# A hybrid attention and state-space trunk step: scaled scores with their extreme in one VectorE pass, and rectified squares of three places on ScalarE

## The chip, the cores and the metric

The kernel runs on one core of a Trainium2 chip. The time is what the device takes for one execution, in microseconds (us), from the first to the last instruction and what lies around them. TensorE (PE) multiplies matrices into PSUM, VectorE (DVE) and ScalarE (ACT) read and write PSUM and SBUF, GpSimd (POOL) works in SBUF, and SyncE (SP) issues most transfers.

## The reference, cut to what matters

One layer of a hybrid encoder: 1024 prompt frames and 64 frames of a running stream, 1,088 columns together, width 1024. Everything is float32; matmuls run on a high part and a low remainder of each operand, three products for one.

```
xn = rmsnorm(x); c_q, c_kv, k_pe, u = split(xn @ w_in)
attention (8 heads, block-causal): s = q k^T * scale; p = softmax(s); out = p v
state space over u: complex diagonal scan, GELU, sigmoid gate
h = x + concat(rmsnorm(attn), rmsnorm(ssm)) @ w_out
h = h + square(relu(rmsnorm(h) @ w_up)) @ w_down       # 1024 -> 4096 -> 1024
y = rmsnorm(h)
```

## The kernel before, in words

The work goes through stages: input projection and state space (to about 330 us), attention of the prompt (334 to 500 us), the gate and the output projection, the norm before the MLP, the up projection (to about 1000 us), the down projection and the final norm.

**Attention.** The loop at line 1299 goes over 64 items (h, i): 8 heads, 8 blocks of 128 queries, in the order `ORD`. Block i sees W = 128 (i + 1) keys, so W is 128 to 1024. `scores(h, i)` (line 1169) makes the scores in a PSUM tile `S` of two banks, of which the pool has two (tag `a`). VectorE then takes the row's maximum over W columns (line 1187) and multiplies that one column by `qsn`, the negative scale of the row (line 1188); the result `nm` is the bias of ScalarE's exponential (line 1190), which reads `S` with the row's scale `qsc`, writes the tile `P` and sums the row. When ScalarE has read `S`, the tile is free for the scores after next. Three items later `back` transposes `P` on TensorE; ScalarE copies the high part out of PSUM (line 1200) and VectorE takes the remainder (`PTl`, line 1201 by the helper at line 51); `values` multiplies with v.

**The up projection** is done by a scheme of seven products instead of eight (`SEQ = "XYXYXZX"`), which add up in three PSUM tiles X, Y and Z. The 4096 rows are cut into 16 sets. `up_evac` (line 1759) empties a tile after each of the seven steps: steps 0 to 2 are copies by ScalarE; steps 3 to 5 add the tile to what was copied (line 1765, VectorE) and then rectify and square it in SBUF (`relu2`, line 1752); step 6 rectifies from PSUM on ScalarE (line 1769), and then line 1773 on VectorE reads the tile in PSUM once more for the square. With `on_act` the squares are two ScalarE instructions (lines 1754 and 1755, and 1771), without it one VectorE instruction, `stt` (line 333). Before the change `on_act` is true for set 2 alone.

The columns come in two chunks of 544. Sets 0 and 1 do their first chunk early (`up_first`) and their second in `up_pair`, ahead of set 9 (`MID`); these tiles are `Xp`, `Yp`, `Zp` and their evacuations have 272 columns. `up_set` does every other set with 544 columns at a time. After a set `up_sums` (line 1775) makes four sums on VectorE and stores seven blocks to HBM on SyncE's queue. That queue, in order, also has the loads of the weights (`wr`, line 1579) and the loads of the stored blocks for the down projection (`rr`, line 1800). The weights go from `wr` through sums (`ws`, VectorE, lines 1604 to 1610) to a high part (ScalarE, line 1618) and a remainder (`wl`, GpSimd, line 51).

**What sets the order.** Parts inside `manual_schedule` (the gate, the start of the MLP up to set 2, the end) keep the order in which they are written. Everything else, attention and sets 3 to 15 among it, is ordered for each engine by a planner when the program is built, from its own estimate of what each instruction takes. Each engine then works through its list in order.

Of the kernel before, what the change touches and what calls it, by code (L numbers as in the profile page):

```python
# [13 lines left out]
AF = mybir.ActivationFunctionType  # L14
ALU = mybir.AluOpType
# [14 lines left out]
def tile_hybrid_step(ctx: ExitStack, tc: tile.TileContext, I: dict, O: dict):  # L30
    nc = tc.nc
    act, dve, pool, pe = nc.scalar, nc.vector, nc.gpsimd, nc.tensor
# [6 lines left out]
    def pg(shape, name, dt=F32):  # L39
        return pages.tile(shape, dt, tag="pg", name=name)  # L40
# [3 lines left out]
    def psb(name):  # L44
        return ps1.tile([128, 512], F32, tag="b", name=name)

    def psa(name):
        return ps1.tile([128, 2, 512], F32, tag="a", name=name, bufs=2)
# [18 lines left out]
    rs = const.tile([128, 9, 8], F32, name="rs")  # L67
    negm = const.tile([128, 9, 8], F32, name="negm")
    qsc = const.tile([128, 9], F32, name="qsc")
    qsn = const.tile([128, 9], F32, name="qsn")  # L70
# [261 lines left out]
    def stt(out, a, s, b, o1, o2):  # L332
        dve.scalar_tensor_tensor(out, a, s, b, op0=o1, op1=o2)  # L333
# [388 lines left out]
    for mt in range(6):  # L722
# [17 lines left out]
        if mt == 4:  # L740
            rt = pg([128, 2, NT], "rot")
# [187 lines left out]
    def head_rows(h):  # L929

        if h % 2 == 0:
            return slice(0, 64), 64, slice(0, 96)
        return slice(64, 128), 32, slice(0, 128)
# [9 lines left out]
    NMP = 0; STP = 1; VHP = 2  # L943
# [16 lines left out]
    for j in range(2):  # L960
        for b in range(2):
            rn, c = slice(64 * b, 64 * b + 64), slice(64 * b, 64 * b + 64)
# [72 lines left out]
    heads, h, wait, v_done = [], 0, 0, False  # L1035
# [59 lines left out]
    for i in range(4):  # L1095
        ps = psb(f"pvc{i}")
        c = slice(128 * i, 128 * i + 128)
# [43 lines left out]
    def p2(shape, dt, name, tag, bufs):  # L1141

        if tag in early:
            return early.pop(tag)
        return ph2.tile(shape, dt, name=name, tag=tag, bufs=bufs)
# [23 lines left out]
    def scores(h, i):  # L1169
        _, _, rk = head_rows(h)  # L1170
        b = h % 2
        W = 128 * (i + 1)
        S = psb(f"S{h}_{i}")[:, None, :] if i in SB else psa(f"S{h}_{i}")
        q = slice(128 * i, 128 * i + 128)
        for bank in range((W + 511) // 512):
            c0 = 512 * bank
            n = min(512, W - c0)
            o = S[:, bank, :n]
            last = c0 + n == W
            pe.matmul(o, lhsT=qT_h[b][rk, q], rhs=kT_h[rk, b, c0:c0 + n], start=True, stop=False)  # L1180
            pe.matmul(o, lhsT=qT_h[b][rk, q], rhs=kT_l[rk, b, c0:c0 + n], start=False, stop=False)
            pe.matmul(o, lhsT=qT_l[b][rk, q], rhs=kT_h[rk, b, c0:c0 + n], start=False, stop=not last)
            if last:
                pe.matmul(S[:, bank, n - 128:n], lhsT=mrow[:, 0:128], rhs=mrow[:, 128:256], start=False, stop=True)
        Sf = S.rearrange("p a c -> p (a c)")[:, 0:W]
        nm = negm[:, i, h:h + 1]
        dve.tensor_reduce(nm, Sf, axis=mybir.AxisListType.X, op=ALU.max)
        (pool if NMP and i < NMP else dve).tensor_scalar(nm, nm, qsn[:, i:i + 1], None, op0=ALU.mult)
        Pt = p2([128, NP], F32, f"P{h}_{i}", "P", 3)
        return Pt, lambda: act.activation(Pt[:, 0:W], Sf, AF.Exp, bias=nm, scale=qsc[:, i:i + 1], accum_out=rs[:, i, h:h + 1])  # L1190

    def transposes(h, i, Pt, PTh, PTl):
        c = slice(128 * (i % 2), 128 * (i % 2) + 128)
# [90 lines left out]
    def flush():  # L1284
        for g in list(later):
            try:
                next(g)
            except StopIteration:
                later.remove(g)
        while ready:  # L1290
            h, i = ready.pop(0)
            if i % 2 == 1:
                values(h, i // 2, *PTs.pop((h, i // 2)), vhs[h])
            if h % 2 == 1 and i == ORD[7]:
                later.append(norm_pair(h // 2))
# [3 lines left out]
    for n, (h, i) in enumerate(items):  # L1299
# [12 lines left out]
        Pt, ex = scores(h, i)  # L1312
# [18 lines left out]
    def rq(shape, name, dt=F32):  # L1331
        return ph3.tile(shape, dt, name=name, tag="rq", bufs=6)
# [103 lines left out]
    NH, NC = NT // 2, NT // 4  # L1436
# [36 lines left out]
    def pump(n=1):  # L1473
        for _ in range(n):
            for g in list(live):
                try:
                    next(g)
                except StopIteration:
                    live.remove(g)
# [87 lines left out]
    MID = 9  # L1567
# [61 lines left out]
    def w_next():  # L1629
        ahead.extend([x for x in [next(wst, None)] if x is not None])  # L1630

    def w_take():
        w = ahead.pop(0)
        w_next()
        return w
# [11 lines left out]
    def step():  # L1647

        todo = later[:]
        later.clear()  # L1650
        for z in todo:
            z()
        pump()
# [92 lines left out]
    def up_product(w, o, i, c, first):  # L1746
        for kt in range(4):
            l = [w[:, x, 128 * kt:128 * kt + 128] for x in range(2)]
            r = [Hop[c][i][:, x, kt] for x in range(2)]
            three(o, l, r, first and kt == 0, kt == 3)  # L1750

    def relu2(z, on_act):
        if on_act:
            act.activation(z, z, AF.Relu)
            act.activation(z, z, AF.Square)
        else:
            stt(z, z, 0.0, z, ALU.max, ALU.mult)

    def up_evac(i, o, z, on_act=False):

        if i in (0, 1, 2):
            act.copy(z(*((0, 0), (1, 1), (1, 0))[i]), o)
        elif i in (3, 4, 5):
            z = z(*((1, 0), (1, 1), (0, 0))[i - 3])
            dve.tensor_tensor(z, o, z, op=ALU.add)  # L1765
            relu2(z, on_act)
        else:
            z = z(0, 1)
            act.activation(z, o, AF.Relu)
            if on_act:  # L1770
                act.activation(z, z, AF.Square)
            else:
                stt(z, o, 0.0, z, ALU.max, ALU.mult)

    def up_sums(b, parts):

        g, k = b // 2, b % 2
        rc, re = rq([128, 2, NH], f"rc{b}"), rq([128, 2, NH], f"re{b}")
        out = rd[g][k]
        for cs, (b11, b21, b12, b22) in parts:  # L1780
            c_, e_ = rc[:, :, cs], re[:, :, cs]
            dve.tensor_tensor(c_[:, 0], b12, b11, op=ALU.subtract)
            dve.tensor_tensor(c_[:, 1], b22, c_[:, 0], op=ALU.subtract)
            dve.tensor_tensor(e_[:, 0], b22, b12, op=ALU.subtract)
            dve.tensor_tensor(e_[:, 1], b21, c_[:, 1], op=ALU.subtract)
            for n, z in ((0, b11), (5, b21), (3, b22)):
                nc.sync.dma_start(out[:, n, cs], z)
            yield
        nc.sync.dma_start(out[:, 1:3], rc)
        nc.sync.dma_start(out[:, 4:7:2], re)  # L1790
# [55 lines left out]
    def up_pair():  # L1846

        rt = [rq([128, 2, 2, NC], f"rb{s_}") for s_ in range(2)]
        made = {}
        for i, x in enumerate(SEQ):  # L1850
            first = x not in made
            if first:
                made[x] = psa(f"{x}p1")
            for s_ in range(2):
                up_product(w_take(), made[x][:, s_, :NC], i, 1, first)
            for s_ in range(2):
                up_evac(i, made[x][:, s_, :NC], lambda k, q: rt[s_][:, k, q])
            pump()
        return rt

    def up_set(b, held=False):
        rt = [rq([128, 2, NH], f"r{x}{b}") for x in "ab"]
        made = {}
        for i, x in enumerate(SEQ):
            w = ahead.pop(0) if held else w_take()
            first = x not in made
            if first:
                made[x] = psa(f"{x}{b}")
            for c in range(2):
                up_product(w, made[x][:, c, :NC], i, c, first)  # L1870
                if held:
                    flush()
                    if c == 0:
                        w_next()
                    step()
            late.append(lambda i=i, x=x: up_evac(i, made[x][:, :, :NC], lambda k, q: rt[k][:, q].rearrange(
                "p (c n) -> p c n", c=2), held))
            if not held:
                flush()
                pump()  # L1880
            if b == 15 and i:
                next(tst)
        flush()
        for _ in up_sums(b, [(slice(0, NH), [t[:, q] for t in rt for q in range(2)])]):
            pass
# [22 lines left out]
    for b in range(3, MID):  # L1908
        up_set(b)
    rt = up_pair()  # L1910
    live.append(pair_sums())
    for b in range(MID, 16):
        up_set(b)
# [30 lines left out]
    for g in range(8):  # L1944
        for jp in range(2):
            if g == 7 and jp == 1:
                break
            made = {}
# [24 lines left out]
    made = [{}, {}]  # L1973
# [319 lines left out]
```

## Time and profile before

| | |
|---|---|
| median of three runs | 1365.03 us (1363.34 to 1367.58) |
| the profiled execution | 1365.45 us, span 1363.3 us |
| mean granted TensorE clock | 0.982 |
| PE busy | 1300.7 us, 95% |
| DVE busy | 1008.7 us, 74% |
| ACT busy | 668.9 us, 49% |
| POOL busy | 641.2 us, 47% |
| moved by DMA | 151.38 MB, mean 111 GB/s |

Busy times are those of one profiled execution; PE's matmuls are pipelined, and the ends that its rows show are modelled. A bracket behind a row of the timeline is how long the engine was idle just before it and what released it.

### The profile page before, as it was taken

Reading aid. Unit: us, or ns where it says so; the run is one execution under the profiler, and the core shown is the slowest. Engines: PE = TensorE matmul, PEld = TensorE weight load, DVE = VectorE, ACT = ScalarE, POOL = GpSimd, SP = SyncE. Lnnn points to the kernel's source line nnn. Section 1 sums busy time; section 2 is a strip of 40 time slices with the busy share of each in tenths; the row PEclk is TensorE's granted clock in tenths of the full one; section 3 lists DMA queues with packets and bytes.
Section 4 is the critical chain, followed back from the end, with each engine's and each line's share of the span. In section 5 each row is a group of like instructions: output and inputs, shape, how many; then the busy total and the mean of one; then the engine's idle time right before and its main releaser. Section 6 shows DMA issues by size and latency. Waiting matters only on the chain.

```text
span 1363.3 us, 24889 instructions
## 1 busy us (share of the span) xinstructions
PE 1300.7 (95%) x9576; PEld 1261.3 (93%) x9576; DVE 1008.7 (74%) x1653; ACT 668.9 (49%) x1333; POOL 641.2 (47%) x626
## 2 busy tenths in 40 slices
PE   6999999989999899999899999899989999999996
PEld 6999998978888789999899999899989999999996
DVE  7679779867788765639965667657587878888756
ACT  6576667756788765214542324232355433343333
POOL 3647556341545516200554546445445446453554
PEclk9999999999999899999999999999999999999998
DMA  6111111210244315124234424443577445664103
GB/s 223 65 41 42 34 30 32 90 49 8 40 86 79 70 65 161 32 96 134 83 115 152 177 97 156 174 169 122 209 252 227 126 154 167 183 180 127 63 1 132
DMA packets 81286, 151.38 MB, mean 111 GB/s; under 512 B 10128, under 2 KB 28816, under 8 KB 81168
## 3 DMA queue, kind: packets, MB, share of 16 engines
q1 hardware_dynamic: 76464, 144.78, 33.5%
q10 hardware_dynamic: 4704, 5.01, 1.1%
q8 instruction: 76, 1.25, 0.4%
q14 instruction: 42, 0.34, 0.1%
HBM read 98.66 MB, written 41.40 MB: 103 GB/s over the span
## 4 chain that ended last, share of the span: by engine, by line
PE 46%; DVE 7%; DMA 4%; POOL 3%; issue 2%; ACT 1%; SPq 0%; DVEq 0%; POOLq 0%; ACTq 0%
PE X L1742 4%; PE X L1744 4%; PE X L1743 4%; PE dX L1742 3%; PE dX L1743 3%; PE dX L1744 3%; PE pw L1494 2%; PE pw L1496 2%; PE pw L1495 2%; POOL wl L51 2%; PE Y L1743 2%; PE Y L1742 2%; PE Y L1744 2%; DMA wr<-in_w_dn_dram 2%; PE dY L1742 2%
## 5 line engine op out<-in xcount | busy, mean ns | idle before, releaser
L51 POOL TENSOR_TENSOR wl<-wr,wl 128x512 fp32r<-128x512 f32 x127 | 196.7, 1557 | 157.3 <-ACT wl L1618 95.3
L51 POOL TENSOR_TENSOR wl<-ws,wl 128x512 fp32r<-128x512 f32 x95 | 146.8, 1546 | 235.6 <-ACT wl L1618 231.2
L1618 ACT CAST wl<-ws 128x512 fp32r<-128x512 f32 x96 | 59.6, 622 | 196.4 <-DVE ws L1606 98.2
L1742 PE MATMUL dX<-to,wl 128*128 128x272 f32 x512 | 149.0, 291 | 3.2 <-DVE q L1939 2.4
L1743 PE MATMUL dX<-to,wl 128*128 128x272 f32 x512 | 147.8, 289 | 0.0
L1744 PE MATMUL dX<-to,wl 128*128 128x272 f32 x512 | 147.5, 288 | 0.0
L1742 PE MATMUL X<-ho,wl 128*128 128x272 f32 x448 | 129.9, 293 | 4.1 <-DVE rb L1765 4.1
L1744 PE MATMUL X<-ho,wl 128*128 128x272 f32 x448 | 130.4, 292 | 0.0
L1743 PE MATMUL X<-ho,wl 128*128 128x272 f32 x448 | 130.2, 291 | 0.0
L1618 ACT CAST wl<-wr 128x512 fp32r<-128x512 f32 x128 | 79.1, 622 | 81.4 <-PE dX L1744 34.0
L1604 DVE TENSOR_TENSOR ws<-wr,wr 128x512 f32<-128x512 f32 x32 | 26.7, 836 | 104.1 <-DMA wr<-in_w_up_dram 63.1
L1742 PEld LDWEIGHTS dX<-to,wl 128*128 128x128 f32 x512 | 96.6, 189 | 4.5 <-DVE q L1939 2.2
L1744 PEld LDWEIGHTS dX<-to,wl 128*128 128x128 f32 x512 | 96.6, 189 | 0.0
L1743 PEld LDWEIGHTS dX<-to,wl 128*128 128x128 f32 x512 | 96.6, 189 | 0.0
L1939 DVE TENSOR_TENSOR q<-dX,q 128x544 f32<-128x544 f32 x108 | 75.9, 717 | 27.7 <-PE dX L1744 27.7
L1742 PEld LDWEIGHTS X<-ho,wl 128*128 128x128 f32 x448 | 85.0, 191 | 4.7 <-DVE rb L1765 4.6
L51 DVE TENSOR_TENSOR to<-rr,to 128x1088 fp32r<-128x1088 f32 x56 | 83.6, 1495 | 4.6 <-ACT to L1813 4.6
L1743 PEld LDWEIGHTS X<-ho,wl 128*128 128x128 f32 x448 | 85.9, 192 | 0.0
L1744 PEld LDWEIGHTS X<-ho,wl 128*128 128x128 f32 x448 | 85.7, 191 | 0.0
L1742 PE MATMUL dY<-to,wl 128*128 128x272 f32 x256 | 74.9, 292 | 4.2 <-DVE ra L333 3.6
L1813 ACT CAST to<-rr 128x1088 fp32r<-128x1088 f32 x56 | 61.7, 1103 | 26.1 <-PE dZ L1744 9.1
L1743 PE MATMUL dY<-to,wl 128*128 128x272 f32 x256 | 74.4, 291 | 0.0
(691 smaller groups left out, 4646.9 us busy)
## 6 DMA issues: line engine op xcount, KB each, us to landing
rr<-rd SPq DMA_DIRECT2D x56, 544.0 KB, 4.8
wr<-in_w_up_dram SPq DMA_DIRECT2D x36, 512.0 KB, 4.7
wr<-in_w_dn_dram SPq DMA_DIRECT2D x32, 512.0 KB, 4.6
rd<-rc SPq DMA_DIRECT2D x16, 544.0 KB, 3.7
rd<-re SPq DMA_DIRECT2D x16, 544.0 KB, 4.3
rd<-ra SPq DMA_DIRECT2D x28, 272.0 KB, 3.1
xw<-in_x_dram SPq DMA_DIRECT2D x8, 544.0 KB, 6.9
hp<-in_x_dram ACTq DMA_DIRECT2D x4, 1088.0 KB, 6.2
```

Source lines behind the costliest of these rows:

```text
L51: eng.tensor_tensor(out, src, hi, op=ALU.subtract)
L1494: pe.matmul(o, lhsT=w[kt][0][:, m_], rhs=rh, start=(kt == 0), stop=False)
L1495: pe.matmul(o, lhsT=w[kt][0][:, m_], rhs=rl, start=False, stop=False)
L1496: pe.matmul(o, lhsT=w[kt][1][:, m_], rhs=rh, start=False, stop=(kt == 3))
L1604: dve.tensor_tensor(s_, a21, a22, op=ALU.add)
L1618: act.copy(w[:, 0], src)
L1742: pe.matmul(o, lhsT=lh, rhs=rh, start=first, stop=False, skip_group_check=True)
L1743: pe.matmul(o, lhsT=lh, rhs=rl, start=False, stop=False, skip_group_check=True)
L1744: pe.matmul(o, lhsT=ll, rhs=rh, start=False, stop=last, skip_group_check=True)
L1813: act.copy(h[:, 0], z)
L1939: dve.tensor_tensor(z, o[:, :, :NC], z, op=ALU.add)
```

## The change

Three edits.

1. In `scores`, the maximum and the small product are replaced by one `tensor_scalar` over the W columns of `S`: it multiplies by `qsn`, writes the product back to `S` in PSUM, and gives the minimum of the products as `nm`. The exponential reads `S` with the constant scale -1.0 in place of `qsc`; what it computes is the same.
2. In `up_pair`, `up_evac` gets `on_act` true: both sets' squares of the second chunk go to ScalarE.
3. In `up_set`, `on_act` is true for sets 9 (`MID`) and 15 too.

```diff
-        dve.tensor_reduce(nm, Sf, axis=mybir.AxisListType.X, op=ALU.max)
-        (pool if NMP and i < NMP else dve).tensor_scalar(nm, nm, qsn[:, i:i + 1], None, op0=ALU.mult)
+        dve.tensor_scalar(Sf, Sf, qsn[:, i:i + 1], None, op0=ALU.mult, op1=ALU.min, accum_out=nm)
         Pt = p2([128, NP], F32, f"P{h}_{i}", "P", 3)
-        return Pt, lambda: act.activation(Pt[:, 0:W], Sf, AF.Exp, bias=nm, scale=qsc[:, i:i + 1], accum_out=rs[:, i, h:h + 1])
+        return Pt, lambda: act.activation(Pt[:, 0:W], Sf, AF.Exp, bias=nm, scale=-1.0, accum_out=rs[:, i, h:h + 1])
...
             for s_ in range(2):
-                up_evac(i, made[x][:, s_, :NC], lambda k, q: rt[s_][:, k, q])
+                up_evac(i, made[x][:, s_, :NC], lambda k, q: rt[s_][:, k, q], True)
...
             late.append(lambda i=i, x=x: up_evac(i, made[x][:, :, :NC], lambda k, q: rt[k][:, q].rearrange(
-                "p (c n) -> p c n", c=2), held))
+                "p (c n) -> p c n", c=2), held or b in (MID, 15)))
```

## Rows read from the trace of the kernel before

**Rows 1.** Windows of attention: length, busy us of PE, PEld, DVE, ACT, POOL, clock, DMA
```profile
334.00:500.00 166.00, 154.28 (x1045) 138.47 (x1046) 129.74 (x289) 126.47 (x294) 71.04 (x107) 0.97 0.30 63
```
**Rows 2.** Waits of the weight loads, 334 to 505 us: total us, times, longest
```profile
PEld S L1180 <- ACT P L1190: 10.8, 15, 2.2
```
**Rows 3.** Timeline of PE where it stood, 830 to 1012 us
```profile
837.62 0.39 PE L1742 MATMUL Xp<-ho,wl 128*128 128x272 f32 x1 [1.57 <-DVE rb L1765]
...
863.15 0.39 PE L1742 MATMUL X<-ho,wl 128*128 128x272 f32 x1 [3.46 <-DVE rb L1765]
...
1004.32 0.60 PE L1742 MATMUL dY<-to,wl 128*128 128x272 f32 x1 [3.60 <-DVE ra L333]
```
**Rows 4.** Windows behind those places, columns as in rows 1
```profile
838.00:842.00 4.00, 4.00 (x34) 4.00 (x33) 4.00 (x8) 1.02 (x2) 1.29 (x1) 1.00 0.22 74
...
864.00:868.00 4.00, 4.00 (x22) 4.00 (x21) 3.93 (x5) 0.01 (x1) 2.73 (x2) 0.57 0.37 139
...
1004.00:1008.00 4.00, 3.68 (x17) 3.68 (x18) 3.96 (x6) 0.55 (x2) 0.76 (x1) 0.57 0.88 239
```
**Rows 5.** The maximum and the small product by line: ns least, median, most
```profile
L1187 DVE TENSOR_REDUCE negm<-S x64: 280/750/1226, 334.5 to 495.4; 128x1 f32<-128x128 f32 x8, 128x1 f32<-128x256 f32 x8, 128x1 f32<-128x896 f32 x8, 128x1 f32<-128x1024 f32 x8
L1188 DVE TENSOR_SCALAR negm<-negm,qsn x64: 196/205/216, 335.3 to 496.4; 128x1 f32<-128x1 f32 x64
```
**Rows 6.** Timeline of DVE: first and last of 41 pairs, 396 to 497 us
```profile
396.25 0.96 DVE L1187 TENSOR_REDUCE negm<-S 128x1 f32<-128x768 f32 x1
...
397.93 0.20 DVE L1188 TENSOR_SCALAR negm<-negm,qsn 128x1 f32<-128x1 f32 x1
...
495.44 0.96 DVE L1187 TENSOR_REDUCE negm<-S 128x1 f32<-128x768 f32 x1 [0.76 <-PE S L1184]
...
496.43 0.21 DVE L1188 TENSOR_SCALAR negm<-negm,qsn 128x1 f32<-128x1 f32 x1
```
**Rows 7.** Waits of ACT, 334 to 505 us, columns as in rows 2
```profile
ACT P L1190 <- DVE negm L1188: 13.2, 25, 1.2
```
**Rows 8.** By line: a read of a row sum, a product into PSUM, a scan
```profile
L1190 ACT ACTIVATION_READ_ACCUMULATOR P<-S,negm,qsc x64: 185/192/227, 350.2 to 497.8; 128x1 f32 x64
L527 DVE TENSOR_TENSOR V<-V,tab x16: 707/720/724, 85.7 to 275.0; 128x542 f32<-128x542 f32 x16
L525 DVE TENSOR_TENSOR_SCAN V<-rt,V x32: 693/716/727, 83.4 to 273.4; 128x271 f32<-128x271 f32 x32
```
**Rows 9.** Squaring on ACT in set 2, by line: us, mean ns, idle before
```profile
L1755 ACT ACTIVATE rb<-rb 128x544 f32<-128x544 f32 x2 | 1.3, 661 | 0.1
```
**Rows 10.** Timeline of DVE in the pair's evacuation
```profile
835.00 1.86 DVE L333 SCALAR_TENSOR_TENSOR rb<-rb 128x272 f32<-128x272 f32 x2
```
**Rows 11.** Timeline of DVE, POOL and SP ahead of the stall in set 9
```profile
844.97 5.64 POOL L51 TENSOR_TENSOR wl<-wr,wl 128x512 fp32r<-128x512 f32 x4
851.19 1.53 DVE L1785 TENSOR_TENSOR re<-rb,rc 128x272 f32<-128x272 f32 x1
852.75 0.37 SPq L1790 DMA_DIRECT2D rd<-re  x1
853.21 0.55 SPq L1579 DMA_DIRECT2D wr<-in_w_up_dram  x1
859.93 0.69 DVE L1604 TENSOR_TENSOR ws<-wr,wr 128x512 f32<-128x512 f32 x1 [3.03 <-DMA wr<-in_w_up_dram]
860.54 0.72 DVE L333 SCALAR_TENSOR_TENSOR rb<-rb 128x544 f32<-128x544 f32 x1
```
**Rows 12.** Timeline of DVE and ACT at set 15
```profile
997.80 1.82 DVE L333 SCALAR_TENSOR_TENSOR rb<-rb 128x544 f32<-128x544 f32 x1
1003.56 0.71 DVE L333 SCALAR_TENSOR_TENSOR ra<-X,ra 128x544 f32<-128x544 f32 x1
997.80 0.62 ACT L1769 ACTIVATE ra<-X 128x544 f32<-128x544 f32 x1
1007.45 0.61 ACT L1942 COPY q<-dY 128x544 f32<-128x544 f32 x1 [5.08 <-PE dY L1744]
```

## The prediction

> **What bounds the kernel now.** The page's first part comes first: TensorE is busy for 95% of the span, VectorE for 74%, ScalarE for 49%. So an edit that takes work off VectorE is worth only what it takes out of TensorE's gaps, and the question is which of these end on an instruction that the change touches. The windows by stage come next. In attention TensorE is busy for 154.3 of 166.0 us, VectorE for 129.7 and ScalarE for 126.5 [rows 1]; none is full, so this stage is a ring of three engines with latency in it. The waits say what ends TensorE's: 15 times, for 10.8 us in all, the scores' weights wait for a tile S that the exponential of an earlier item still has to read [rows 2]. In the up projection I followed TensorE's timeline for brackets. It stands three times where the change is made: 1.57 us in the pair and 3.46 us in set 9, both until VectorE has added a tile, and 3.60 us at the first down product, until a `stt` has read set 15's last tile [rows 3]. The windows behind them have a second price: after the 3.46 and the 3.60 us the granted clock was 0.57 over four us, so about 0.43 x 4 = 1.7 us of work at 2.4 GHz was lost to the 1.2 GHz level each time; after the 1.57 us it was 1.00 [rows 4]. These gaps make the sum.
>
> **The change, part by part: the scores.** It removes 64 maxima, 0.280 us at 128 columns and 1.226 at 1024, and 64 products of one column at 0.205, which are 13.1 us [rows 5]. From the two ends a maximum costs (1.226 - 0.280) / 896 = 1.056 ns a column and 0.145 us fixed. It adds 64 passes that read and write PSUM, and a way to get the minimum out. What it takes away above all is a place in the queue: the small product needs the maximum's result, and the planner puts other work between the two. Over the 41 pairs from 396 us on, the time from the end of the maximum to the end of the product is 0.63 us in the mean; in the first it is 398.13 - 397.21 = 0.92, in the last, where nothing stands between, 0.24 [rows 6]. 18 of these 41 exponentials begin within 0.25 us of the product's end, and ScalarE stood for just that product 25 times, 13.2 us [rows 7].
>
> No row has a VectorE pass that gives a row result beside its output, so I bound it. For the read-out the nearest row is ScalarE's own read of a row sum, 0.192 us; the ends are 0 and 0.63, as late as now. I take 0.2. For the pass the low end is the maximum's rate: a product with input and output in PSUM took 0.720 us for 542 columns, so writing there costs nothing visible (0.145 + 542 x 1.056 ns = 0.717). The high end is the scan, which also carries a value from column to column: 0.716 for 271 columns, that is (0.716 - 0.145) / 271 = 2.11 ns [rows 8]. I take the maximum's rate, since the maximum carries a value too and is the row with the same result. Then VectorE does as much as before (13.1 us out, 64 x 0.2 = 12.8 in), and an exponential that waits comes 0.63 - 0.2 = 0.43 us earlier. I apply that to the share 18 / 41 of the 15 waits: 15 x 0.44 x 0.43 = 2.8 us. The ends are 0 and all 10.8 us, before the slow pass, which is a rival.
>
> The Trainium skill speaks against "one pass" here (VectorE: DVE Perf Modes, section Two Vector instructions with no wait between them): an operation that writes out its accumulator is two instructions, the main one and a read. No run here shows that on VectorE; ScalarE's row shows it there. Were it one, the gain would be 15 x 0.44 x 0.63 = 4.1 in place of 2.8 us.
>
> **The squares.** Each `relu2` on ScalarE is two instructions of about 0.66 us at 544 columns [rows 9], and less at 272. The pair sends 8 `stt` away and adds 14 instructions of 272 columns; sets 9 and 15 send 4 away each and add 7 of 544 columns, 7 x 0.66 = 4.6 us each.
>
> *Pair.* Ahead of the addition that ends the 1.57 us wait VectorE runs two `stt` for 1.86 us [rows 10]; with them gone the addition starts before TensorE asks. ScalarE covers the added instructions: it was busy for 1.02 of the 4 us from 838 on [rows 4]. Without that cover the wait stays.
>
> *Set 9.* Here one must follow a chain. The addition came late since a weight sum at 859.93 stood before it in VectorE's queue for 3.03 us until its load landed. That load was issued at 853.21, behind a store at 852.75 in SyncE's queue, and the store waited for the pair's sum that ran on VectorE from 851.19 to 852.72. The `stt` that go from VectorE before it are the two of 1.86 us and six more, which at the rate of rows 5 are 0.145 + 272 x 1.056 ns = 0.43 us each: over 4 us of its queue. The load cannot go ahead by all of that: GpSimd read the buffer it fills until 844.97 + 5.64 = 850.61, so by 853.21 - 850.61 = 2.6 us. The `stt` at 860.54 goes too: 0.6 us [rows 11]. So the addition comes 3.2 us earlier. TensorE reaches it 1.57 us earlier too, so of 1.57 + 3.46 us the pair and set 9 give back 3.2 together, and the wait that remains, 1.8 us, is between the one that lowered the clock and the one that didn't: half of 1.7. Together 3.2 + 0.9 = 4.1 us; the ends are 0.6 (only that `stt`) and 1.57 + 3.46 + 1.7 = 6.7.
>
> *Set 15.* Now ScalarE rectifies the last tile out of PSUM at 997.80, and VectorE reads it again at 1003.56, behind a `stt` of 1.82 us and remainders of the down projection's operands. Afterwards the rectifying alone frees the tile, at 998.42 plus what is put before it on ScalarE. Step 5's two squares surely are, 1.3 us: 999.7, and TensorE came to its gap at 1004.32 - 3.60 = 1000.72, so it doesn't stand. If the squares of steps 3 to 5 all are, 4.0 us, it waits until 1002.4, 1.8 of 3.6 us. ScalarE has room behind, 5.08 us idle before 1007.45 [rows 12]; what comes late next there is a copy or a weight's high part by some 0.6 us, and I take that off: 3.6 + 1.7 - 0.6 = 4.7 us, the ends 1.8 and 5.3. The sums and stores of set 15 are needed only by the last group of the down projection.
>
> The skill gives a reason for the long `stt` (SBUF — State Buffer, on the shared port pair): a VectorE instruction with two SBUF inputs and a GpSimd one that reads SBUF exclude each other, and the later one waits in full. The trace agrees: the same `stt` took 0.72 us at 860.54 [rows 11] and 1.82 at 997.80 [rows 12]. By the rule the squares that leave VectorE give GpSimd time too; I take nothing for it.
>
> **Sum.** 2.8 + 4.1 + 4.7 = 11.6 us off the profiled execution's 1365.45 us: 1353.85. That execution is 0.42 above the median of the runs, so 1353.4 us.
>
> **Rivals.** *The pass runs at the scan's rate* (slower). 64 items have 8 x 4,608 = 36,864 columns; 1.05 ns more for each is 38.8 us more for VectorE, whose attention load becomes 129.7 + 38.8 - 0.3 = 168.2 us in a stage of 166. Of its 36.3 idle us some stay; with half of them the stage takes 186.3, 20.3 more, and against the 8.8 us from the squares the kernel takes 1365.03 + 20.3 - 8.8 = 1376.5. It decides from where attention grows by 8.8 us: VectorE at 156.7, 0.43 us more in each pass. For it: a value carried through a product, as in the scan. Against it: the maximum.
> *The ring doesn't notice*: the exponential is early, but waits for ScalarE's own list; only the squares count: 1365.03 - 8.8 = 1356.2.
> *The waits of the up projection come back on ScalarE*: the squares stand ahead of the high parts of the weights and TensorE waits for those: 1365.03 - 2.8 = 1362.2. For it: ScalarE makes every weight's high part. Against it: its idle time at all three places.
> *Another order*: attention and the sets are in an order that the planner works out anew from other instructions. Two new places like set 15's, 3.6 + 1.7 us each, would leave 1353.4 + 10.6 = 1364.0.
>
> **How the numbers follow.** Forecast 0.47; no gain in attention 0.14; waits back on ScalarE 0.15; another order 0.12; slow pass 0.12. A change under 0.3%, 4.1 us, can't be told from none: faster is below 1360.9, slower above 1369.1. Faster: 0.47 + 0.14, with 0.03 of the third and 0.04 of the order's: 0.68. Same: 0.12 + 0.05 = 0.17. Slower: 0.12 and 0.03 of the order's: 0.15. The range starts at 1344, just inside the upper ends of all three parts (1365.03 - 10.8 - 6.7 - 5.3 = 1342.2), and ends at 1371, short of the slow pass's own time.
>
> **What would show it.** In attention: passes of 0.28 to 1.23 us with a read of about 0.2 behind each, ScalarE's waits on `negm` below 13.2 us, and TensorE's on the exponential near 8 us in place of 10.8; a pass near 2 us at 1024 columns is the first rival. In the up projection: no bracket in the pair, one of at most 2 us in set 9 with its load issued nearer 850, none at the first down product, and a clock near 1.00 behind it. The forecast is wrong if brackets of the same length stand there with ScalarE as their releaser, or if attention takes more than 166 us.

## The result, and the profile after

The changed kernel takes 1350.96 us (median of four runs, 1347.35 to 1353.54) where the kernel before took 1366.30 beside it: ratio 0.9895, 95% interval 0.9869 to 0.9922. In a second series it was 1351.26, ratio 0.9893 (0.9879 to 0.9907). The forecast was 1353.4. The profiled execution took 1347.35 us (span 1345.6), 18.1 less than that of before; it is the fastest of its four. The parts behind the sum came out otherwise: about 9.7 us from edit 1, where I had 2.8, and 4.8 from the squares, where I had 8.8. Two errors of opposite sign made a good sum.

The windows of the changed kernel; the first stretch is that of [rows 1], with 7.6 us of the gate already in it; the second ends where attention does:

```profile
334.00:500.00 166.00, 157.30 (x1110) 144.18 (x1110) 132.93 (x298) 123.89 (x303) 74.11 (x109) 1.00 0.32 68
334.50:492.40 157.90, 149.20 (x1063) 136.15 (x1062) 129.71 (x291) 119.87 (x294) 71.53 (x107) 1.00 0.32 67
```

From the first masked product of the scores to the gate's first product attention takes 157.9 us; before it was 502.1 - 334.2 = 167.9. The clock of this execution is 1.00 throughout, 0.97 in [rows 1].

The new pass by shape (count, total us, mean ns, idle before it), beside [rows 5]:

```profile
L1188 DVE TENSOR_SCALAR_CACHE_REDUCE S<-S,qsn 128x1024 f32<-128x1024 f32 x8 | 10.3, 1289 | 0.9 <-PE S L1184 0.8
L1188 DVE DVE_READ_ACCUMULATOR S<-S,qsn 128x1 f32 x64 | 8.8, 138 | 0.1
...
L1188 DVE TENSOR_SCALAR_CACHE_REDUCE S<-S,qsn 128x128 f32<-128x128 f32 x8 | 2.7, 338 | 1.4 <-PE S L1184 1.3
```

(1.289 - 0.338) / 896 = 1.06 ns a column: the maximum's rate, and 0.06 us more fixed. The read takes 0.138 us and stands right behind the pass, as VectorE's timeline shows:

```profile
475.05 1.16 DVE L1188 TENSOR_SCALAR_CACHE_REDUCE S<-S,qsn 128x896 f32<-128x896 f32 x1
476.12 0.14 DVE L1188 DVE_READ_ACCUMULATOR S<-S,qsn 128x1 f32 x1
```

The result is there 0.05 us after the pass's row ends, and 0.06 us in the mean of all 64 items. Before, it took 0.63 us in the mean of the 41 pairs of [rows 6] and 0.61 in that of all 64. The Trainium skill's rule that an accumulator's output is an instruction of its own (VectorE: DVE Perf Modes, section Two Vector instructions with no wait between them) agrees with these rows.

The waits in attention, 334 to 505 us (total us, times, longest), beside [rows 2, 7]:

```profile
ACT P L1190 <- DVE S L1188: 12.9, 17, 1.6
PEld S L1180 <- ACT P L1190: 7.6, 8, 1.6
```

ScalarE waits less often for the extreme, 17 times for 25, but hardly less in all (12.9 us for 13.2). TensorE's weight loads wait 3.2 us less for the exponential.

What I hadn't counted is that the exponential itself became shorter. By shape, first before, then after:

```profile
L1190 ACT ACTIVATE P<-S,negm,qsc 128x1024 f32<-128x1024 f32 x8 | 9.7, 1209 | 1.8 <-DVE negm L1188 1.8
...
L1190 ACT ACTIVATE P<-S,negm,qsc 128x128 f32<-128x128 f32 x8 | 3.7, 465 | 0.0
```

```profile
L1190 ACT ACTIVATE P<-S,negm 128x1024 f32<-128x1024 f32 x8 | 9.0, 1120 | 0.6 <-DVE S L1188 0.3 <-DVE PTl L51 0.3
...
L1190 ACT ACTIVATE P<-S,negm 128x128 f32<-128x128 f32 x8 | 2.9, 366 | 2.4 <-POOL wg L51 1.2 <-DVE S L1188 1.1
```

At every width 0.08 to 0.10 us went, 64 times: 5.7 us of ScalarE.

TensorE's brackets in the up projection and behind it, beside [rows 3]:

```profile
824.89 0.39 PE L1742 MATMUL X<-ho,wl 128*128 128x272 f32 x1 [0.49 <-DVE rb L1765]
825.73 0.39 PE L1742 MATMUL Y<-ho,wl 128*128 128x272 f32 x1 [0.33 <-ACT wl L1618]
850.00 0.40 PE L1742 MATMUL X<-ho,wl 128*128 128x272 f32 x1 [1.93 <-DVE rb L1765]
979.80 0.39 PE L1742 MATMUL X<-ho,wl 128*128 128x272 f32 x1 [1.23 <-DVE rb L1765]
1000.82 0.40 PE L1742 MATMUL dX<-to,wl 128*128 128x272 f32 x1 [1.76 <-DVE q L1939]
```

In place of the pair's wait of 1.57 us stand two of 0.49 and 0.33, set 9's is 1.93 in place of 3.46, and the 3.60 us at `dY` are gone. (That `dY` is not the first down product, as I called it: in the kernel before `dX` products run from 990.55 us on.) A wait of 1.76 us is new, for VectorE's sum `q`. It stands 18 us behind set 15's last `X` product, where that of `dY` stood 7 us behind it. The windows behind these places have the full clock, where [rows 4] had 0.57 twice:

```profile
850.00:854.00 4.00, 4.00 (x31) 4.00 (x32) 1.45 (x3) 3.69 (x8) 2.58 (x2) 1.00 0.18 70
984.00:988.00 4.00, 4.00 (x34) 4.00 (x33) 4.00 (x3) 4.00 (x9) 3.44 (x3) 1.00 0.53 158
998.00:1002.00 4.00, 2.24 (x18) 2.02 (x17) 3.76 (x5) 0.82 (x2) 1.09 (x1) 1.00 1.05 400
```

The last of these shows the transfers at the new wait: the share of the 16 engines is 1.05.

### The profile page after: what moved, and what is told of

Same layout as the page of the kernel before. It is cut to its first block, busy times and chain, and to the rows that moved or that the text cites. A ratio compares the mean times of both kernels' runs of the same rounds, so it can differ in the third digit from the quotient of the medians.

```text
span 1345.6 us, 24897 instructions
## 1 busy us (share of the span) xinstructions
PE 1288.5 (96%) x9576; PEld 1251.8 (93%) x9576; DVE 1000.2 (74%) x1637; ACT 673.7 (50%) x1361; POOL 640.3 (48%) x626
## 4 chain that ended last, share of the span: by engine, by line
PE 71%; DVE 10%; POOL 5%; DMA 5%; issue 4%; ACT 4%; SPq 0%; DVEq 0%; ACTq 0%; POOLq 0%
PE X L1742 4%; PE X L1744 4%; PE X L1743 4%; PE dX L1742 3%; PE dX L1744 3%; PE dX L1743 3%; PE pw L1494 2%; POOL wl L51 2%; PE pw L1495 2%; PE pw L1496 2%; PE pq L207 2%; PE pq L208 2%; PE pq L209 2%; PE Y L1743 2%; PE Y L1742 2%
```

## The experiments

Each was timed in five rounds beside the kernel before on the same chip, in three series. The kernel before had a median of 1363.26 us in the series of the first four rows below, 1364.10 in that of `pair_only`, `set9_only` and the two `after_pool` runs, and 1365.47 in that of the other four, so ratios are to be compared, not medians.

| run | median, us | ratio to before | 95% |
|---|---|---|---|
| scores_only | 1353.97 | 0.9929 | 0.9913 to 0.9946 |
| squares_only | 1359.00 | 0.9965 | 0.9952 to 0.9977 |
| const_scale | 1358.53 | 0.9964 | 0.9952 to 0.9976 |
| fused_row_scale | 1356.60 | 0.9944 | 0.9928 to 0.9959 |
| fused_hop | 1361.54 | 0.9976 | 0.9964 to 0.9987 |
| pair_only | 1361.46 | 0.9986 | 0.9971 to 1.0001 |
| set9_only | 1362.15 | 0.9986 | 0.9971 to 1.0001 |
| set15_only | 1361.85 | 0.9973 | 0.9959 to 0.9988 |
| after_stores | 1349.44 | 0.9888 | 0.9872 to 0.9904 |
| after_again | 1351.26 | 0.9893 | 0.9879 to 0.9907 |
| after_pool_g1 | 1355.74 | 0.9936 | 0.9913 to 0.9959 |
| after_pool_odd | 1354.38 | 0.9928 | 0.9902 to 0.9954 |

### The two halves

**Edit 1 alone** (the diff's first part):

> Edit 1 alone; the squares stay as before. The trace of the changed kernel reaches the gate's first product 9.7 us earlier than before and the first full set 11.1 us earlier. Theory A (edit 1 did all of that): 10 to 11 us faster than before, ratio 0.992 to 0.993, the gate's first product near 492, no clock below 1.00 between 464 and 492 us. Rival (my prediction's term, the rest being the order that all three edits together gave): 2.8 us faster, ratio 0.998.

0.0071 of 1363.26, 9.7 us: theory A's number, three and a half times my term. The clock from 454 to 494 us fell all the same in this execution (0.87 and 0.96), so that part of the expectation missed.

Not all of it lies in attention. In the profiles, attention takes 159.7 us for 167.9, the stretch from the gate's first product to the first full set 158.2 for 161.1, and the sets 332.0 for 333.8; the work ahead of attention took 3.9 us longer. With the squares as before, the waits in the pair and in set 9 are 2.29 and 0.27 us, for 1.57 and 3.46 [rows 3]:

```profile
832.66 0.39 PE L1742 MATMUL Xp<-ho,wl 128*128 128x272 f32 x1 [2.29 <-DVE rb L1765]
...
856.51 0.39 PE L1742 MATMUL X<-ho,wl 128*128 128x272 f32 x1 [0.27 <-DVE rb L1765]
```

Each compute engine's order in these sets is that of before. So the squares alone don't fix the length of set 9's wait. Counted from the product that waited in the pair, its load landed 1.9 us sooner (the sum ahead of it took VectorE 0.43 us, for 1.53 in [rows 11]), and TensorE came to the wait 1.5 us later, after a clock of 0.76 and 0.81 over the 8 us from 832 on. What made that sum short was not tried.

**Edits 2 and 3 alone:**

> Edits 2 and 3 alone; attention as before. My prediction's terms: 4.1 + 4.7 = 8.8 us faster, ratio 0.9936. What the trace of the changed kernel shows from the first full set to the end: 17.7 - 11.1 = 6.6 us, ratio 0.9952; PE's brackets near 1.9 us in set 9, 1.2 us in set 15, 1.8 us early in the down projection. Rival (the squares gain nothing, the start of the sets only moves): within 2 us of before.

4.8 us (3.1 to 6.5), below my 8.8 and within what the revised figure allows. 9.7 + 4.8 = 14.5 us, and together they gave 14.3 to 14.6: the halves add up. In attention the three edits have no order of their own together: by the traces each engine's order there is in `scores_only` that of the changed kernel, and in `squares_only` that of before.

### What in edit 1 does it

```diff
-dve.tensor_scalar(nm, nm, qsn[:, i:i + 1], None, op0=ALU.mult)
-... AF.Exp, bias=nm, scale=qsc[:, i:i + 1]
+dve.tensor_scalar(nm, nm, -0.01, None, op0=ALU.mult)
+... AF.Exp, bias=nm, scale=0.01
```

> Before, with the exponential's scale a constant (0.01) and the small product by a constant (-0.01) too: maximum and small product both stay, in their places; left out is the row's own scale. In the changed kernel an exponential of 1024 columns took 1.120 us of ScalarE in place of 1.209, and 128 columns 0.366 in place of 0.465. Theory A (what counts is that the extreme comes earlier): exponentials 0.09 us shorter, time 0 to 2 us below before (at most the 24 waits of TensorE for an exponential, 0.09 us each). Theory B (the shorter exponential is the larger part of attention's 10 us): 5 us or more faster, ratio 0.996 or less. Rival to both (the exponential's length comes from its input and not from its scale): no change of its length, and none of the time.

This kernel leaves out the row's own scale. 4.9 us: just short of theory B's number and well above A's. The exponentials are 0.09 us shorter, as expected. The small product turned out shorter too, 0.145 us in the median in place of the 0.205 of [rows 5], its factor no longer being a column. That is 0.15 us of instructions an item; the way from the scores to a free tile, measured below, became 0.27 us shorter. TensorE's weight loads wait as often as before for the exponential, for less each time:

```profile
PEld S L1180 <- ACT P L1190: 7.2, 15, 1.2
```

The other way round, the fused pass with a column as scale (edit 1, and `qsm` is a column of -1.0):

```diff
-... scale=-1.0
+... scale=qsm[:, 0:1]
```

> Edit 1 alone, but the exponential takes its scale of -1 from a column in SBUF, as before, and not as a constant. Theory A: exponentials back at 0.465 to 1.209 us, and still 8 us or more faster than before, ratio 0.994 or less. Theory B: at most 5 us faster, ratio 0.996 or more.

7.6 us; the exponential of 1024 columns is back at 1212 ns. Attention takes 494.8 - 335.3 = 159.5 us in its profile and 497.8 - 338.1 = 159.7 with edit 1 whole: behind the fused pass the shorter exponential is worth some 2 us by the medians, whose intervals overlap, and nothing by the two profiles. So each alone gives a good part, and they don't add: 4.9 and 7.6, together 9.7.

Then the place in the queue:

```diff
 dve.tensor_scalar(Sf, Sf, qsn[:, i:i + 1], None, op0=ALU.mult, op1=ALU.min, accum_out=nm)
+dve.tensor_scalar(nm, nm, 1.0, None, op0=ALU.mult)
```

> Edit 1 alone, with the small step put back: behind the fused pass VectorE multiplies the one column by 1.0, and the exponential waits for that. Theory A (what edit 1 gains is the place in VectorE's queue between the extreme and the exponential): most of the fused pass's own part is lost again; with the shorter exponential left, no more than the 5 us of the constant scale alone, ratio 0.996 or more, and as VectorE has 13 us more to do, perhaps less. Rival (the gain comes from the order that the planner gives a fused pass, or from the pass itself): 8 us or more faster still, ratio 0.994 or less.

3.3 us are left of 9.7. One instruction of 0.144 us, put between the extreme and the exponential, takes back two thirds of the gain, and TensorE's wait is near its old 10.8 [rows 2] again, here in the waits of that kernel:

```profile
ACT P L1191 <- DVE negm L1189: 18.4, 27, 1.4
PEld S L1180 <- ACT P L1191: 10.5, 21, 1.8
```

This agrees with theory A: what counts is how soon the extreme reaches ScalarE. From the end of the pass to the end of the small product it is 0.63 us in the mean of the 64 items, as between maximum and product before (0.61); in 52 of the 64 items (49 before) other work stands between the two in VectorE's list, while the read stands right behind its pass. The timing alone can't tell this from the 64 x 0.144 = 9.2 us that VectorE has more to do.

A rival stands beside all three. The planner makes a new order for each of these kernels: in attention the order of TensorE, VectorE and ScalarE in `const_scale`, `fused_row_scale`, `fused_hop` and `scores_only` is not that of before. So each time is that of an edit with its order. What a new order gives by itself, with the instructions as they were, was not tried.

### What the squares do

> Edit 2 alone. The chain of my prediction (sums of the pair, a store, a weight's load, a weight sum, the addition of set 9): the squares of the pair are what the load of set 9 waits for, so the pair alone shortens both brackets: the pair's from 1.57 to under 0.7 and set 9's from 3.46 to 2 to 2.5, 2 to 4 us faster, ratio 0.997 to 0.9985. Rival (each edit mends its own place alone): the pair's bracket gone and set 9's at 3.4 us or longer, as TensorE is earlier there: within 1 us of before.

1.9 us in the timing (-0.1 to 4.0), which can't be told from nothing. The trace has the chain as predicted: no wait of TensorE in the pair but 0.32 us for ScalarE, the load of set 9's weight issued at 848.41 where [rows 11] have 853.21, and this bracket in set 9:

```profile
860.89 0.49 PE L1742 MATMUL X<-ho,wl 128*128 128x272 f32 x1 [2.38 <-DVE rb L1765]
```

> Edit 3 for set 9 alone. The chain: the load is as late as before, only one squaring of 0.6 us goes from in front of the addition; the pair's bracket stays at 1.5 and set 9's at 2.8 to 3.5 us; at most 1 us faster, ratio 0.999 or more. Rival (set 9's own squares are what it waits for): its bracket below 2 us, 2 us or more faster.

1.9 us again, with the same interval. The brackets are as the chain has them, 1.50 in the pair and 3.15 in set 9. But look at the clock behind set 9's bracket, first with set 9 alone and then with the pair alone:

```profile
866.00:870.00 4.00, 4.00 (x34) 4.00 (x33) 2.36 (x4) 3.28 (x7) 2.34 (x2) 1.00 0.39 123
```

```profile
862.00:866.00 4.00, 4.00 (x25) 4.00 (x24) 3.93 (x5) 0.28 (x1) 2.46 (x2) 0.70 0.41 146
```

TensorE kept the 2.4 GHz level behind the wait of 3.15 us, and lost it in part behind the wait of 2.38 us.

> Edit 3 for set 15 alone. My prediction's term: 4.7 us faster, ratio 0.9966, nothing late but a ScalarE copy by 0.6. Revised by the trace of the changed kernel: 3.6 + 1.7 less a new wait of 1.8 us of the first dX for VectorE's sum, 3.5 us, ratio 0.9974. Rival (what it gives at the first down product is given back behind it): within 1 us of before, ratio 0.9993 or more.

3.7 us (1.6 to 5.6), the revised number. The profiled execution was the slowest of its twelve; the wait at `dY` is gone there too, and another of almost its length stands at a later `dX`:

```profile
1015.19 0.60 PE L1742 MATMUL dX<-to,wl 128*128 128x272 f32 x1 [3.35 <-DVE q L1939]
```

### The waits that are left

```diff
-        nc.sync.dma_start(out[:, 1:3], rc)
-        nc.sync.dma_start(out[:, 4:7:2], re)
+        eng = nc.scalar if b in (0, 1, 15) else nc.sync
+        eng.dma_start(out[:, 1:3], rc)
+        eng.dma_start(out[:, 4:7:2], re)
```

> The changed kernel, with the stores of the four sums of the pair and of set 15 issued by ScalarE and no longer in SyncE's queue. Theory S (the waits left, 1.93 us in set 9 and 1.76 us at dX in the down projection, come from loads that stand in SyncE's queue behind a store that waits for VectorE's sums): both brackets below 1 us, 2 to 3.5 us faster than the changed kernel, ratio to before 0.987 to 0.988. Rival 1 (the chain over the weight sum, its high part and GpSimd's remainder sets them): brackets as they are, the same time within 1 us. Rival 2 (ScalarE is held by the stores' own waits): new brackets with a weight's high part as releaser, slower than the changed kernel by 1 us or more.

Theory S falls. 0.9888 and the changed kernel's 0.9893 can't be told apart, and both brackets stand in the trace with their releasers:

```profile
852.37 0.39 PE L1742 MATMUL X<-ho,wl 128*128 128x272 f32 x1 [1.78 <-DVE rb L1765]
...
1004.74 0.39 PE L1742 MATMUL dX<-to,wl 128*128 128x272 f32 x1 [1.98 <-DVE q L1940]
```

> The changed kernel once more, beside the others on the same chip: 0.9895 of before, as in its first runs, 0.987 to 0.992. The clock from 454 to 494 us, 1.00 in the first profile and 0.87 to 0.96 with edit 1 alone: if the clock is settled by the kernel it is 1.00 again; if it also falls by chance at the same short waits, it may be lower here.

The same time as the first time, but another clock. In attention both executions have three short waits at the same products, 0.34, 1.33 and 0.50 us in the first and 0.34, 1.46 and 0.50 in the second. The windows behind them, first then second execution:

```profile
468.00:472.00 4.00, 3.60 (x32) 3.47 (x31) 2.69 (x8) 3.41 (x8) 4.00 (x6) 1.00 0.01 2
```

```profile
470.00:474.00 4.00, 4.00 (x19) 3.85 (x18) 1.53 (x3) 1.86 (x4) 4.00 (x6) 0.50 0.00 0
```

One program, almost the same waits: 1.00 the one time, 0.50 the other.

```diff
-                lo_sub(dve, h[:, 1], z, f(h[:, 0]))
+                lo_sub(pool if g == 1 else dve, h[:, 1], z, f(h[:, 0]))
```

> The changed kernel, with the seven remainders of the down projection's second group of operands on GpSimd in place of VectorE. Theory V (the first dX waits for VectorE's sum since an operand's remainder, which waits for its load, stands in front of it in VectorE's queue): the bracket of 1.8 to 2.9 us there goes below 1 us, 1 to 3 us faster than the changed kernel, ratio to before 0.987 to 0.989. Rival 1 (a weight sum that waits for its own load stands there as well): the bracket stays, time as the changed kernel's. Rival 2 (GpSimd's weight remainders come late behind the new work): brackets with a remainder as releaser, slower than the changed kernel.

The bracket near 1001 us is gone, as theory V has it; but 25 us later, where the changed kernel's profile has one of 1.26 us, one of 3.73 us stands with the same releaser, and the time is worse than the changed kernel's, 0.9936 against 0.9893 in the series before:

```profile
1025.96 0.60 PE L1742 MATMUL dX<-to,wl 128*128 128x272 f32 x1 [3.73 <-DVE q L1939]
```

The second form has `pool if g < 2 and i % 2 else dve` there:

> The same for every second operand of the first two groups. Theory V: half of the remainders are out of VectorE's way and it gets through the last set's sums earlier, at the first dX a bracket of 1 to 2 us; 0 to 2 us faster than the changed kernel, ratio to before 0.988 to 0.9895. Rival 2: the operands of the first group come late from GpSimd, new brackets before 995 us, slower than the changed kernel by 1 us or more.

0.9928, by its median slower than the changed kernel too, though the intervals touch, with eight brackets of 0.2 to 1.8 us between 850 and 1030 us. No version that I ran is measurably faster than the changed kernel.

## Why the prediction was right, and where it wasn't

**The pass and the read: right.** The rate is the maximum's. The read came out at 0.138 us (I took 0.2), the pass at 0.06 us more than the maximum. VectorE has as much to do as before: 64 x 0.2 + 36,864 x 1.06 ns + 8.8 = 61 us, against 48 + 13.1. The slow-pass rival is out.

**Attention's 2.8 us: the step that failed.** It was "I apply that to the share 18 / 41 of the 15 waits": I priced the weight loads' waits for an exponential and nothing else, and the term was too small by a factor of three. To see what was missing, split attention's length into TensorE's idle time, what the lower clock cost (in windows of 2 us, busy time by one less the granted clock) and the rest. The last column is the way: from the end of the masked product of an item's scores to the end of its exponential, which frees the tile, in the mean of the 64 items.

| profiled execution | length | idle | lost to the clock | rest | way |
|---|---|---|---|---|---|
| before | 167.9 | 11.7 | 4.9 | 151.3 | 3.46 |
| fused_hop | 166.6 | 10.1 | 1.7 | 154.8 | 3.46 |
| const_scale | 161.9 | 7.4 | 3.2 | 151.3 | 3.19 |
| fused_row_scale | 159.5 | 7.6 | 1.6 | 150.3 | 3.06 |
| scores_only | 159.7 | 8.1 | 3.3 | 148.3 | 3.01 |
| changed kernel | 157.9 | 8.7 | 0.0 | 149.2 | 3.00 |
| changed kernel, again | 160.0 | 8.1 | 3.3 | 148.6 | 3.02 |

The nearest test of my term is `fused_row_scale`, the fused pass with an exponential as long as before. There the weight loads' waits for the exponential are these:

```profile
PEld S L1182 <- ACT P L1192: 8.6, 12, 1.7
```

That is 2.2 us less than the 10.8 of [rows 2], so the price of these waits was about right. But attention became 8.4 us shorter: all of TensorE's idle time fell by 4.1, the clock's cost by 3.3, and 1.0 is rest. So the first thing missing is the other idle time that goes with a shorter way. In the changed kernel the idle time fell by 3.0 to 3.6 us; that this is near 2.8 is luck in part, since `const_scale`, without the pass, takes off 4.3.

Second, the clock: 0.97 over 166 us in [rows 1] is 5 us, the dearest number of that row, and I used it in the up projection only. In the kernel before, TensorE was busy for 1.99 of the 4 us from 464 and for 2.05 of those from 484, and the clock behind was 0.56 and 0.62. Five profiles with that attention (before, squares_only and the three places alone) lost 4.5 to 5.1 us to it; of six with the whole of edit 1, five lost 3.3 and the first one nothing. So some 1.6 us are the edit's, and 3.3 more of the first profile's 10.0 are luck.

Third, the exponential with a constant scale; alone, with its shorter small product and its order, it is worth as much as half of edit 1's gain.

The lengths follow the way: the three kernels with 3.4 us and more, squares_only among them (3.47 and 168.0), have 166.6 us and more, the others 162 and less. That is why the two savings don't add: together they take 0.45 us off the way, alone 0.27 and 0.40. The rest is 2 to 3 us lower with the whole of edit 1 and 3.5 higher in `fused_hop`, which I can't place. That matmuls' ends are modelled may be a part of it, and so may the order.

The Trainium skill has the third as a price: each column operand adds some 93 ns to an ACTIVATE (ScalarE: Activation LUTs, section What ACT_TABLE_LOAD costs). The rows give 0.08 to 0.10 us, so they agree. I read the new line as "what it computes is the same" and asked nothing about its time.

**Pair and set 9: the chain right, the sum not as I had it.** I said 1.8 us would remain in set 9; it is 1.93, and 1.95 and 1.74 in two other profiles. What holds it now, in the changed kernel's timelines, one fence for several engines:

```profile
836.83 0.32 SPq L1789 DMA_DIRECT2D rd<-rc  x1
837.99 0.55 SPq L1579 DMA_DIRECT2D wr<-in_w_up_dram  x1
...
844.43 0.69 DVE L1604 TENSOR_TENSOR ws<-wr,wr 128x512 f32<-128x512 f32 x1 [0.78 <-DMA wr<-in_w_up_dram]
...
847.31 1.28 POOL L51 TENSOR_TENSOR wl<-ws,wl 128x512 fp32r<-128x512 f32 x1 [6.42 <-ACT wl L1618]
848.62 0.69 DVE L1608 TENSOR_TENSOR ws<-wr,ws 128x512 f32<-128x512 f32 x1 [1.47 <-POOL wl L51]
849.23 0.72 DVE L1765 TENSOR_TENSOR rb<-X,rb 128x544 f32<-128x544 f32 x1
```

The load lands, VectorE sums, GpSimd takes the remainder of that sum, and only then may VectorE overwrite it; the addition stands behind. So moving the stores away didn't help. From the first full set's first product to set 15's last, the stage takes 330.4 us after and 333.8 before. These 3.4 us are near my 4.1, but 1.8 of them are there with edit 1 alone (332.0), where set 9's wait is 0.27. Beside that kernel the squares gave nothing in the length of these waits: 2.29 + 0.27 us without them, and 0.49, 0.33 and 1.93 with them. What they gave there is the clock, 0.76 and 0.81 behind the pair's wait in `scores_only` and 1.00 behind each wait in the changed kernel, one execution each. In `squares_only`, where attention is as before, the stage takes 330.1, 3.7 less. The timing gives less, 4.8 - 3.7 = 1.1 with several us of doubt. So the chain is right for the order of events in the kernel that I read, and its sum is right by luck in part. The 0.9 us for a clock that falls half as far behind half the wait has no ground: the two windows above contradict it.

**Set 15: the tile right, what follows wrong.** ScalarE rectified the last tile at 984.17 and had it free at 984.78, with one pass of step 5's square put right ahead of it; TensorE didn't stand and kept its clock. But "what comes late next there is a copy or a weight's high part by some 0.6 us" failed. What comes late is VectorE's `q`, by 1.76 us (2.94 in the second execution, 3.35 with set 15 alone):

```profile
997.10 1.10 ACT L1813 CAST to<-rr 128x1088 fp32r<-128x1088 f32 x1 [2.72 <-DMA rr<-rd]
998.24 1.29 DVE L51 TENSOR_TENSOR to<-rr,to 128x1088 fp32r<-128x1088 f32 x1 [2.38 <-ACT to L1813]
...
1000.05 1.35 DVE L1939 TENSOR_TENSOR q<-dX,q 128x544 f32<-128x544 f32 x2
```

The operand's load is late for ScalarE by 2.72 us, its remainder waits on VectorE, and the sum that frees `dX` stands behind it. Taking the remainder out of the way moved the wait and didn't end it. That the transfers are the limit there is read from their share of 1.05, and not tried by itself. Measured, set 15 is worth 3.7 us of 4.7 (1.6 to 5.6), with an order of the down products behind it that the planner made anew.

**The rivals.** In the changed kernel no bracket of more than 0.33 us has ScalarE as its releaser in the up projection, so the waits didn't come back there. "The ring doesn't notice" is refuted by edit 1 alone. New waits did come, 1.76 us at a `dX` and 0.5 more in set 15 (1.23 for 0.69), some 2.3 of the 10.6 us that the rival of another order priced. Its condition came true, since attention has another order; its cost didn't come.

## What to carry to other kernels

Where a ring of engines is bound by latency, measure the whole way round it, with what waits in the queues between its instructions and its operands' form included. Here one instruction of 0.144 us put back made the way 0.45 us longer and the kernel 6.4 us slower, and 0.15 us less of instructions made it 0.27 us shorter and the kernel 4.9 us faster, each with the order that the planner then chose. Read the granted clock of the same stretch before summing waits; a clock of 0.97 is a term of its own, but a saving by it in one execution may be chance. A wait behind a load can change by microseconds though nothing near it was edited, so look at it in more than one kernel before pricing it. And when an edit lets TensorE reach a stage sooner, look up which load that stage starts from, since the load need not be sooner.

## What the runs showed of the hardware

- A column in place of a constant as the scale cost ScalarE's exponential 0.08 to 0.10 us at every width. On VectorE the one-column product took 0.205 us with a column as factor [rows 5] and 0.145 with a constant.
- VectorE's pass with a result beside its output was two instructions here, a pass at the maximum's rate (1.06 ns a column) and a read of 0.138 us.
- Almost the same short waits of one program left TensorE at 2.4 GHz in one execution and at 1.2 GHz for some us in another, and a wait of 3.15 us left it alone where one of 2.38 us didn't.
